# Third buffers, keys a head ahead, squares summed on TensorE, and a new woven order in a fused GDN, sparse-attention and MLP layer

## The chip, the cores and the metric

One core of a Trainium2 chip runs the whole layer in one launch. The metric is device time in microseconds (us) of an execution; lower is better. Five engines run side by side, each through its own instructions in order: PE (TensorE, matmuls), ACT (ScalarE), DVE (VectorE), POOL (GpSimd) and SP (SyncE, which issues most transfers).

## The reference, cut to what matters

One decoder block over 1024 positions of width 1024. The piece that the change touches is the gated DeltaNet branch (GDN): 8 heads of 128, chunks of tokens, a short causal convolution, l2-normalised q and k, a decay, and a triangular solve.

```python
h = rms_norm(x, norm_mix_g)
proj = h @ w_in
qkv = silu(causal_short_conv(g_qkv, conv_w))          # 4 taps
gq = l2_normalize(gq) * 128 ** -0.5                   # x * rsqrt(sum(x*x) + EPS)
gk = l2_normalize(gk)
beta = sigmoid(g_b); g = -exp(a_log) * softplus(g_a + dt_bias)
decay = exp(g_cum[i] - g_cum[j])                      # i >= j
a_mat = (k_beta @ k.T) * decay                        # i > j
sol = triangular_solve(I + a_mat, [v * beta, k_beta * exp(g_cum)])
for each chunk n:                                     # the scan
    v_new = u_n - w_n @ state
    o_n = q_n @ state + qk_n @ v_new
    state = state * exp(g_last) + k_n.T @ v_new
o_gdn = rms_norm(o_gdn) * silu(z)
o_att = sparse attention over the 256 best keys of an indexer
x = x + (sigmoid(gate_a) * o_gdn + sigmoid(gate_b) * o_att) @ w_out
x = x + relu(rms_norm(x) @ w_mlp_up) ** 2 @ w_mlp_down
```

## The kernel before, in words

**Tiling and stages.** Tokens are cut into 8 blocks of 128 (`NB`, `P`). The core first normalises x, then projects the indexer, the attention operands and the decay scalars (the start, about the first 270 us), then runs the GDN heads with the indexer's top-k search beside them (to about 1000 us), the attention, the output projection, and from about 1258 us the MLP.

**The dense stream.** The GDN weights are cut into 48 units (`gunits`, L659): for each head k, q, v (convolved), z and gate a, and for all heads gate b. `gload` (L668) fetches a unit's raw weights, `gweights` (L674) splits them on ACT and DVE into a high and a low part (tiles `w`), and `gdense` (L696) runs 2 halves of 24 matmuls each of 128x512 into PSUM tiles `dd`. A half may begin only when the same half of the unit before has been drained, by `conv` or `gate`, on ACT (`cu<-dd`, `th<-dd`). These matmuls are the filler of the order: anything else that PE has to do is put between them.

**A head's chain.** `conv` (L745) copies the two halves into `cu` (2 buffers), scales and adds the four taps (`kt`, `qt` or `t`), takes tanh into `cu` on ACT and finishes silu on DVE. From k, `keys` (L786) fetches the cumulated decay into `es` by a broadcast DMA (`es<-GC`), transposes the eight blocks of k on PE (`tt<-kt`, `tt<-ident,kt`), takes the sum of squares of each with an ACT Square that accumulates (`gj,kss<-tt`) and the decayed keys `kd` with a second ACT instruction, turns `es` into the decay with ACT's Abs and Exp (`es<-es,ngc`), and makes the matrix `am`. POOL then inverts the 32x32 diagonal blocks in 31 steps (`stmp`, `sx`), with two round trips through DRAM (`ZA`, `ZU`) into `um`. `join` (L887) puts the blocks together with small matmuls (`jj`). From q, `queries` (L941) transposes 8 blocks only to sum squares in the same way (`qss`), then multiplies k and q into `es`. `values` (L975) transposes v (`vv`), `scan` (L997) runs 8 dependent steps (`cc`, `oo`, `sr`, `svn`, `sst`) and `output` (L1050) norms and gates the result. `es`, `kd` and `um` have two buffers each, so `keys` of head h waits for the scan of head h-2 before it does anything.

**What sets the order.** Nothing is ordered by hand. Every piece is a generator chain with a priority (`wv.add`), and `Weave` (L1608) plays the chains against a model of durations (`__getattr__`, L1694) and issues whichever may run. `issue` (L1622) ties each instruction to the one before it on its engine, so that the order planned at build time is the order on the chip: an instruction whose data come later than planned holds up everything behind it on its engine. All instructions carry the line of that wrapper, L1699, so that a reader goes by tile names.

Of the kernel before, what the change touches and what calls it, by code (L numbers as in the profile page):

```python
# [20 lines left out]
P = 128  # L21
# [8 lines left out]
TOPK = 256  # L30
NEG = -1.0e30
# [18 lines left out]
def body(tc, a, out, dbg=None):  # L50
# [67 lines left out]
    cmask = cst.tile([P, P], F32, name="cmask")  # L118
    vecs = cst.tile([P, NV], F32, name="vecs")
    g025 = cst.tile([P, 1], F32, name="g025")  # L120
    dtb = cst.tile([P, H], F32, name="dtb")
# [25 lines left out]
    def loads():  # L147
        SY_.dma_start(ident, a["c_ident"])
        after(("ident",))
        for half in range(2):  # L150
            if half == 0:
                ts = [ix.tile([P, NB, 256], F32, name="pj", bufs=2).rearrange("p a b -> p (a b)") for _ in range(2)]
                xs.extend(t[:, o:o + D] for t in ts for o in (0, D))
            else:
                xs.extend([slot(1, [P, D], F32), slot(5, [P, D], F32)]
                          + [ix.tile([P, D], F32, name="irl", bufs=2) for _ in range(2)])
            for tb in range(4 * half, 4 * half + 4):
                SY_.dma_start(xs[tb], x[tb * P:(tb + 1) * P, :])
# [15 lines left out]
        G_.memset(ones, 1.0)  # L174
        SY_.dma_start(ropeA, a["c_ropea"])
        SY_.dma_start(qng, a["q_norm_g"].to_broadcast([P, P]))
        SY_.dma_start(kng, a["k_norm_g"].to_broadcast([P, P]))
        SY_.dma_start(cmask, a["c_mask"])
        yield
# [418 lines left out]
    def select():  # L598
# [29 lines left out]
        for qb in range(2):  # L628
            m = scp.tile([P, 2, P], BF16, name="tkcm")
            G_.memset(m[:, 0, :], 0.0)  # L630
            G_.tensor_copy(m[:, 1, :], cmask)
            yield
            SY_.dma_start(MK[qb, :, :(qb + 1) * P], m[:, 1 - qb:, :])
# [21 lines left out]
    gunits = []  # L655
# [6 lines left out]
    graws = [None, None]  # L662

    def wtile(kind, u):
        i = {"r": (2, 3), "h": (6, 0), "l": (7, 4)}[kind][u % 2]
        return slot(i, [P, KT, P], F32 if kind == "r" else F32R)

    def gload(u):  # L668
        h, c = gunits[u]
        c0 = cstart[c] + h * P  # L670
        graws[u % 2] = wtile("r", u)
        SY_.dma_start(graws[u % 2], w_in[:, c0:c0 + P].rearrange("(k p) c -> p k c", p=P))

    def gweights():  # L674
        yield ("pdense", len(units) - 2)
        gload(0)
        gload(1)
        for u in range(len(gunits)):
            yield
            if u == 1:  # L680
                yield ("pdense", len(units) - 1)
            if u > 1:
                yield ("dense", u - 2)
            yield "A"
            hi, lo = wtile("h", u), wtile("l", u)
            A_.activation(hi, graws[u % 2], AF.Copy)
            yield
            yield "V"
            V_.tensor_tensor(lo, graws[u % 2], hi.bitcast(F32), op=OP.subtract)
# [55 lines left out]
    def conv(u):  # L745
# [14 lines left out]
        if c == "k" and h > 2:  # L760
            yield ("out", h - 3)
        if c == "q" and h > 1:
            yield ("scan", h - 2)
        if c == "v" and h:
            yield ("values", h - 1)
# [14 lines left out]
        yield  # L780
        wv.done("conv", u)
        st[h][c + "t"] = o
# [3 lines left out]
    def keys(h):  # L786
        kt = st[h]["kt"]
        if h > 1:
            yield ("scan", h - 2)
        kd = gp.tile([P, NB, P], F32, name="kd", bufs=2)  # L790
        es = gp.tile([P, NB, P], F32, name="es", bufs=2)
        am = gq.tile([P, NB, P], F32, name="am", bufs=2)
        um = gp.tile([P, NB, P], F32, name="um", bufs=2)
        kss = gp.tile([P, NB], F32, name="kss", bufs=2)
# [3 lines left out]
        for half in range(2):  # L798
            yield tt.ready
            ps, slot_ = tt.get()  # L800
            for i in range(4):
                PE_.transpose(ps[:, i, :], blk(kt, half * 4 + i), ident)
            yield
            for i in range(4):
# [4 lines left out]
                if i % 2:  # L809
                    yield  # L810
            tt.free(slot_)
# [8 lines left out]
        ke = gp.tile([P, NB], F32, name="ke", bufs=2)  # L820
        V_.tensor_scalar(ke, kss, 4 * EPS, None, op0=OP.add)
        yield
        yield from rsq_w(gp, rk, ke, NB, "rk")
# [29 lines left out]
        st[h].update(kd=kd, aq=es, am=am, av=av, nb=nb_, um=um)  # L853
# [32 lines left out]

    def join(h):  # L887
# [8 lines left out]
        ys = gq.tile([P, NB, 32], F32, name="ys", bufs=1)  # L896
# [26 lines left out]
        y6 = gq.tile([64, NB, 64], F32, name="y6", bufs=1)  # L923
# [17 lines left out]
    def queries(h):  # L941
        qt = st[h]["qt"]
        yield ("keys", h)
        if h > 1:
            yield ("out", h - 2)
        kt, aq = st[h]["kt"], st[h]["aq"]
        qss = gp.tile([P, NB], F32, name="qss", bufs=2)
        for half in range(2):
            hs = slice(half * 4, half * 4 + 4)
            yield tt.ready  # L950
            ps, slot_ = tt.get()
            for i in range(4):
                PE_.transpose(ps[:, i, :], blk(qt, half * 4 + i), ident)
            yield
            for i in range(4):
                b = half * 4 + i
                junk = gp.tile([P, P], BF16, name="gj")
                A_.activation(junk, ps[:, i, :], AF.Square, accum_out=qss[:, b:b + 1])
                if i % 2:
                    yield  # L960
            tt.free(slot_)
# [9 lines left out]
        st[h]["qss"] = qss  # L971
        wv.done("queries", h)
# [24 lines left out]
    def scan(h):  # L997
        yield ("queries", h)
        yield ("values", h)
        if h:  # L1000
# [49 lines left out]
    def output(h):  # L1050
# [4 lines left out]
        V_.tensor_scalar(fe, qss, 4 * EPS, 128 * EPS, op0=OP.add, op1=OP.mult)  # L1055
# [52 lines left out]
    xslot = (1, 5, 2, 3, 6, 7, 0, 4)  # L1108
# [72 lines left out]
    def wout_weights():  # L1181
        free = [("V", 1), ("out", H - 1), ("w", last), ("w", last), ("dense", last - 1), ("dense", last - 1)]
# [425 lines left out]
class Weave:  # L1608
    def __init__(self, tc):
        self.tc, self.now, self.idle, self.t = tc, 0.0, 0.0, 0.0  # L1610
        self.busy, self.last, self.ev, self.chains = {}, {}, {}, []
# [10 lines left out]
    def issue(self, name, ins, dur, lat):  # L1622
# [5 lines left out]
        end = max(self.busy.get(name, 0.0), self.now) + dur  # L1628
# [61 lines left out]
class _Ordered:  # L1690
    def __init__(self, wv, eng, name):
        self.wv, self.eng, self.name = wv, eng, name

    def __getattr__(self, op):  # L1694
# [3 lines left out]
        def call(*args, **kw):  # L1698
# [5 lines left out]
            if name == "PE":  # L1704
# [3 lines left out]
                if op == "matmul" and "tile_position" in kw:  # L1708
                    return wv.issue(name, ins, 0.03, 0.25)
                return wv.issue(name, ins, (n * (0.417 if fast else 0.835) + 2.5) / 1e3, 0.25)  # L1710
            if name == "SY":
                return wv.issue(name, ins, max(0.5, n * o.shape[0] / 9e4), SY_LATENCY)
            if name == "A":
                return wv.issue(name, ins, 0.13 + n / 1200 + (0.1 if "accum_out" in kw else 0), 0.15)
            if name == "V":
                return wv.issue(name, ins, 0.07 + n / 960, 0.12)
            if op == "tensor_tensor":
                return wv.issue(name, ins, 0.33 + n / 476, 0.2)
            return wv.issue(name, ins, 0.15 + n / 1000, 0.2)
# [3 lines left out]
def constants():  # L1723
# [4 lines left out]
    c["c_mask"] = np.where(i[None, :] <= i[:, None], 0.0, NEG).astype(np.float32)  # L1728
# [42 lines left out]
```

## Time and profile before

| what | before |
|---|---|
| median of 3 runs | 1967.49 us (1966.48 to 1968.16) |
| the profiled execution, its own time | 1966.45 us |
| its span | 1964.7 us |
| mean granted clock of TensorE | 0.987 of full speed |
| PE, DVE, ACT, POOL busy | 1917.2, 1045.0, 890.6, 374.3 us |
| instructions | 27845, of them 10526 on PE |

PE's rows are records of matmuls: a float32 product of two 128x128 tiles leaves two records, a transpose one. Their ends are modelled and overlap, so that the distance from one start to the next tells more than a mean duration. A stretch in which PE's clock falls from 1.00 to 0.50 runs its matmuls at half speed. The time between span and execution, 1.75 us, lies around the span.

### The profile page before, as it was taken

To read this page: it belongs to the slowest core of one execution; us is meant where nothing else is said; L and a number is where in the kernel's file an instruction comes from. 1 tells how busy PE (TensorE), PEld (TensorE's weight loads), DVE (VectorE), ACT (ScalarE), POOL (GpSimd) and SP (SyncE) were. 2 spreads that over 40 slices of the span, in tenths; PEclk is the share of its full clock that TensorE was granted. 3 is DMA by queue.
4 is the path that set the end of the run, shared out by engine and by line. 5 is a ranking of instruction groups with operands and counts; after the bars stand their busy time and mean duration, and the time that the engine had idled before them with its cause. 6 is when DMAs were issued, how large, how long until landed. Compare 5 with 4: busy or idle time off the path is not lost.

```text
span 1964.7 us, 27845 instructions
## 1 busy us (share of the span) xinstructions
PE 1917.2 (98%) x10526; PEld 1613.2 (82%) x10526; DVE 1045.0 (53%) x2371; ACT 890.6 (45%) x2022; POOL 374.3 (19%) x661
## 2 busy tenths in 40 slices
PE   8899999999999799999999999999999999999999
PEld 7899988887887688888877888788888888888887
DVE  4547767767868786543377766623223232223222
ACT  6556657657655535543365655532221314132220
POOL 0214721540650533531021221000000000000000
PEclk9999999998999899999999999999999999999999
DMA  4111243212322222223362211212020211112012
GB/s 152 45 43 44 83 122 60 65 47 62 64 58 46 60 71 78 56 69 92 97 221 92 71 61 49 76 38 59 32 81 17 70 43 43 48 38 60 32 33 91
DMA packets 181689, 131.17 MB, mean 67 GB/s; under 512 B 34306, under 2 KB 161715, under 8 KB 181555
## 3 DMA queue, kind: packets, MB, share of 16 engines
q1 hardware_dynamic: 181554, 129.40, 23.1%
q8 instruction: 82, 1.34, 0.3%
q14 instruction: 53, 0.43, 0.1%
HBM read 107.18 MB, written 22.18 MB: 66 GB/s over the span
## 4 chain that ended last, share of the span: by engine, by line
PE 93%; DVE 3%; ACT 3%; DMA 1%; issue 1%; SPq 0%; ACTq 0%; DVEq 0%
PE dd L1699 58%; PE o L1699 11%; PE pt L1699 11%; PE s L1699 3%; PE tt L1699 3%; PE cc L1699 2%; PE jj L1699 2%; PE sq L1699 2%; PE oo L1699 1%; DVE rqs L1699 1%; ACT pr L1699 1%; DVE sc L1699 0%; PE tp L1699 0%; DMA es<-GC 0%; DMA pj<-in_x_dram 0%
## 5 line engine op out<-in xcount | busy, mean ns | idle before, releaser
L1699 PE MATMUL dd<-hh,w 128*128 128x512 f32 x1568 | 526.6, 407 | 2.6 <-ACT cu L1699 1.6
L1699 PEld LDWEIGHTS dd<-hh,w 128*128 128x128 f32 x1568 | 292.5, 190 | 59.6 <-ACT cu L1699 2.8
L1699 PE MATMUL dd<-hl,w 128*128 128x512 f32 x784 | 319.1, 407 | 0.9 <-DVE hl L1699 0.9
L1699 PE MATMUL dd<-w,hh 128*128 128x256 f32 x960 | 181.6, 286 | 0.0
L1699 PEld LDWEIGHTS dd<-hl,w 128*128 128x128 f32 x784 | 149.2, 190 | 28.1 <-DVE hl L1699 1.2
L1699 ACT ACTIVATE dh<-dr 128x512 fp32r<-128x512 f32 x64 | 40.2, 628 | 280.3 <-PE o L1699 230.4
L1699 PEld LDWEIGHTS dd<-w,hh 128*128 128x128 f32 x960 | 153.0, 192 | 1.5
L1699 ACT ACTIVATE rl<-dd 128x512 f32<-128x512 f32 x64 | 38.3, 598 | 218.6 <-PE dd L1699 218.6
L1699 PE MATMUL dd<-w,hl 128*128 128x256 f32 x480 | 137.0, 285 | 0.0
L1699 POOL TENSOR_TENSOR stmp<-sx,um 128x60 f32<-128x60 f32 (+24 forms) x248 | 109.9, 443 | 99.0 <-DMA sx<-in_c_xinit_dram 80.8
L1699 DVE TENSOR_TENSOR w<-w,o 128x512 f32<-128x512 f32 x64 | 44.0, 688 | 126.4 <-PE o L1699 126.4
L1699 DVE TENSOR_SCALAR_CACHE_REDUCE tkeq<-sc,cand 128x384 f16<-128x384 f32 (+3 forms) x128 | 103.5, 808 | 1.5
L1699 PE MATMUL dd<-h2h,uh 128*128 128x512 f32 x256 | 100.7, 393 | 1.3 <-DVE w L1699 1.3
L1699 POOL TENSOR_TENSOR sx<-sx,stmp 128x60 f32<-128x60 f32 (+24 forms) x248 | 98.2, 396 | 19.4
L1699 PE MATMUL dd<-hh,ul 128*128 128x512 f32 x256 | 100.4, 392 | 0.0
L1699 PE MATMUL dd<-h2l,uh 128*128 128x512 f32 x256 | 100.4, 392 | 0.0
L1699 PE MATMUL dd<-hh,uh 128*128 128x512 f32 x256 | 100.3, 392 | 0.0
L1699 PE MATMUL dd<-h2h,ul 128*128 128x512 f32 x256 | 100.3, 392 | 0.0
L1699 PE MATMUL dd<-hl,uh 128*128 128x512 f32 x256 | 100.3, 392 | 0.0
L1699 DVE TENSOR_TENSOR w<-w,pt 128x512 f32<-128x512 f32 x64 | 44.0, 688 | 102.1 <-PE pt L1699 101.0
L1699 PEld LDWEIGHTS dd<-w,hl 128*128 128x128 f32 x480 | 91.9, 191 | 0.1
L1699 DVE TENSOR_TENSOR dl<-dr,dh 128x512 fp32r<-128x512 f32 x64 | 44.0, 688 | 84.3 <-ACT dh L1699 84.3
(366 smaller groups left out, 4384.4 us busy)
## 6 DMA issues: line engine op xcount, KB each, us to landing
w<-in_w_in_dram SPq DMA_DIRECT2D x48, 512.0 KB, 3.9
ur<-in_w_mlp_up_dram SPq DMA_DIRECT2D x32, 512.0 KB, 4.3
dr<-in_w_mlp_down_dram SPq DMA_DIRECT2D x64, 256.0 KB, 2.8
wraw<-in_w_in_dram SPq DMA_DIRECT2D x8, 1024.0 KB, 5.3
w<-in_x_dram SPq DMA_DIRECT2D x10, 512.0 KB, 5.1
es<-GC SPq DMA_DIRECT2D x8, 512.0 KB, 9.1
um<-ZA SPq DMA_DIRECT2D x32, 128.0 KB, 3.9
M<-kt SPq DMA_DIRECT2D x8, 512.0 KB, 2.8
```

What stands on the lines that cost most here:

```text
L1699: ins = f(*args, **kw)
```

## The change

- **Buffers.** `es` gets a third buffer; the third `um`, for every third head, takes the large slot 3. For that the raw GDN weights get one slot (2) instead of two (2, 3): a unit's weights are now fetched when the unit before it has been split. The decayed keys with their k transposes become a chain of their own, `decayed`. `keys` now waits for the scan of head h-3 and the join of head h-2.
- **Units.** The k unit of each head goes a head ahead in `gunits`, and two gate b units (`EARLY`) go behind head 0's.
- **Squares.** The accumulating ACT Squares of k (64) and q (64) and the 64 transposes of q go. In their place `conv` of k and of q squares the whole tile in one ACT instruction into `cu`, and PE multiplies each of its 8 blocks, as the stationary operand, by a 128x1 column of ones; a DVE addition of EPS takes the sums out of PSUM.
- **The planner.** Its price of a matmul column goes from 0.417 to 0.441 ns, the fixed part from 2.5 to 5 ns, wide small matmuls cost 0.06 us, two POOL prices fall slightly, and DVE and POOL instructions with two operands in SBUF are planned one after another (`port`).
- **Smaller ones.** The causal mask is made on POOL rather than loaded, `ys` and `y6` of `join` live in free blocks of `am`, and the slots in which the attention and the output weights wait are renumbered.

```diff
...
-    for h in range(H + 1):
-        gunits += [(h, c) for c in "kqv" if h < H] + [(h - 1, c) for c in "za" if h]
-    gunits += [(h, "b") for h in range(H)]
+    gunits = [(0, "k"), (0, "q"), (0, "v"), (1, "k")]
+    for h in range(H):
+        gunits += [(g, c) for g, c in ((h + 1, "q"), (h + 1, "v"), (h + 2, "k")) if g < H] + [(h, "z"), (h, "a")]
+        if h == 0:
+            gunits += [(g, "b") for g in range(EARLY)]
+    gunits += [(h, "b") for h in range(EARLY, H)]
...
-        i = {"r": (2, 3), "h": (6, 0), "l": (7, 4)}[kind][u % 2]
+        i = {"r": (2, 2), "h": (6, 0), "l": (7, 4)}[kind][u % 2]
...
-            if u + 2 < len(gunits):
-                gload(u + 2)
+            if u + 1 < len(gunits):
+                gload(u + 1)
...
+        st[h][c + "t"] = o
+        if c != "v":
+            yield "A"
+            A_.activation(cu[:, 0:S], o, AF.Square)
+            yield
+            yield tt.ready
+            ps, slot_ = tt.get()
+            for b in range(NB):
+                PE_.matmul(ps[:, 0, b:b + 1], blk(cu, b), one, start=True, stop=True)
+            yield
+            st[h][c + "ss"] = gp.tile([P, NB], F32, name=c + "ss", bufs=3)
+            V_.tensor_scalar(st[h][c + "ss"], ps[:, 0, 0:NB], 4 * EPS, None, op0=OP.add)
+            tt.free(slot_)
+            yield
         wv.done("conv", u)
...
     def keys(h):
         kt = st[h]["kt"]
+        if h > 2:
+            yield ("scan", h - 3)
         if h > 1:
-            yield ("scan", h - 2)
-        kd = gp.tile([P, NB, P], F32, name="kd", bufs=2)
-        es = gp.tile([P, NB, P], F32, name="es", bufs=2)
+            yield ("join", h - 2)
+        es = gp.tile([P, NB, P], F32, name="es", bufs=3)
-        um = gp.tile([P, NB, P], F32, name="um", bufs=2)
-        kss = gp.tile([P, NB], F32, name="kss", bufs=2)
+        um = slot(3, [P, NB, P], F32) if h % 3 == 2 else gp.tile([P, NB, P], F32, name="um", bufs=2)
+        wv.add(3, decayed(h))
...
-                A_.activation(junk, ps[:, i, :], AF.Square, accum_out=kss[:, b:b + 1])
-                A_.activation(kd[:, b, :], ps[:, i, :], AF.Copy, scale=egd[:, b, h:h + 1])
...
+    def decayed(h):
+        if h > 1:
+            yield ("scan", h - 2)
+        kd = gp.tile([P, NB, P], F32, name="kd", bufs=2)
+        for half in range(2):
+            yield tt.ready
+            ps, slot_ = tt.get()
+            for i in range(4):
+                PE_.transpose(ps[:, i, :], blk(st[h]["kt"], half * 4 + i), ident)
+            yield
+            for i in range(4):
+                b = half * 4 + i
+                A_.activation(kd[:, b, :], ps[:, i, :], AF.Copy, scale=egd[:, b, h:h + 1])
...
     def queries(h):
...
-                PE_.transpose(ps[:, i, :], blk(qt, half * 4 + i), ident)
-            yield
-            for i in range(4):
-                b = half * 4 + i
-                junk = gp.tile([P, P], BF16, name="gj")
-                A_.activation(junk, ps[:, i, :], AF.Square, accum_out=qss[:, b:b + 1])
...
-                    return wv.issue(name, ins, 0.03, 0.25)
-                return wv.issue(name, ins, (n * (0.417 if fast else 0.835) + 2.5) / 1e3, 0.25)
+                    return wv.issue(name, ins, 0.03 if n <= 32 * NB else 0.06, 0.25)
+                return wv.issue(name, ins, (n * (0.441 if fast else 0.835) + 5) / 1e3, 0.25)
...
```

**The order on PE, where head 1 is joined.** Before (`dd` are the dense matmuls, `jj` those of the join, `tt<-ident,vv` the transposes of v, `cc<-vv,um` the first step of head 1's scan, x4 stands for four alike):

```order
L1699 MATMUL jj<-ys,t_4976 32x32 x16
L1699 MATMUL jj<-t_4976,ys 32x32 x8
L1699 MATMUL dd<-hl_1_124,w_4701 128x512
L1699 MATMUL dd<-hh_1_108,w_4702 128x512
L1699 MATMUL jj<-um,am 64x64 x8
L1699 MATMUL jj<-y_5092,t_4976 64x64 x8
L1699 MATMUL tt<-ident,vv 128x128 x4
L1699 MATMUL cc<-vv,um 128x128
L1699 MATMUL tt<-ident,vv 128x128 x4
L1699 MATMUL cc<-svn,kd 128x128
L1699 MATMUL oo<-svn,es 128x128
L1699 MATMUL dd<-hh_0_93,w_4876 128x512
```

With the change, where the scan of head 0 ends and head 1 is joined (`tt<-one,cu` are the new sums of squares):

```order
L1727 MATMUL cc<-sr,um 128x128
L1727 MATMUL oo<-svn,es 128x128
L1727 MATMUL tt<-ident,kt 128x128 x8
L1727 MATMUL jj<-um,am 32x32 x16
L1727 MATMUL jj<-am,t_4978 32x32 x16
L1727 MATMUL jj<-t_4978,am 32x32 x8
L1727 MATMUL jj<-um,am 64x64 x8
L1727 MATMUL jj<-am,t_4978 64x64 x8
L1727 MATMUL tt<-one,cu 128x1 x8
L1727 MATMUL tt<-ident,vv 128x128 x4
L1727 MATMUL cc<-vv,um 128x128
L1727 MATMUL dd<-hh_0_93,w_4706 128x512
```

The last dense matmul ahead of this piece stands six rows earlier; the piece begins with the last step of head 0's scan, then come the output's transposes, the whole join, a burst of ones and the first step of head 1. Before, dense matmuls of one unit lay between the join's steps; now there is none up to the last row.

**The order on PE, where head 3's v is transposed.** Before (`tt<-ident,kt` is the output of the head before, `cc` and `oo` are steps of the scan):

```order
L1699 MATMUL dd<-hh_1_108,w_6937 128x512
L1699 MATMUL cc<-sst,kt 128x128
L1699 MATMUL oo<-sst,qt 128x128
L1699 MATMUL cc<-sr,um 128x128
L1699 MATMUL oo<-svn,es 128x128
L1699 MATMUL tt<-ident,kt 128x128 x8
L1699 MATMUL tt<-ident,vv 128x128 x4
L1699 MATMUL dd<-hh_0_93,w_7184 128x512
```

With the change:

```order
L1727 MATMUL tt<-ident,vv 128x128 x4
L1727 MATMUL dd<-hh_1_108,w_7278 128x512
L1727 MATMUL jj<-am,t_7528 32x32 x16
L1727 MATMUL jj<-t_7528,am 32x32 x8
L1727 MATMUL dd<-hl_1_124,w_7278 128x512
L1727 MATMUL dd<-hh_1_108,w_7279 128x512
L1727 MATMUL dd<-hh_0_93,w_7450 128x512
L1727 MATMUL dd<-hl_0_109,w_7450 128x512
```

Before, six rows stand between two dense matmuls; now the transposes of v and two steps of a join stand between dense matmuls.

**The order on ACT, ahead of head 4's decay** (`es<-es,ngc` is its Abs, `kd<-tt,egd` the decayed keys, `gj,kss<-tt` the squares of k, `cu<-qt` and `cu<-kt` the tanh of a convolution or the new square, `svn<-cc` and `gj,oss<-vv` steps of a scan). Before:

```order
L1699 ACTIVATE gj,kss<-tt 128x128
L1699 ACTIVATE kd<-tt,egd 128x128
L1699 ACTIVATE um<-jj 64x8x64
L1699 ACTIVATE gj,kss<-tt 128x128
L1699 ACTIVATE kd<-tt,egd 128x128
L1699 ACTIVATE gj,kss<-tt 128x128
L1699 ACTIVATE kd<-tt,egd 128x128
L1699 ACTIVATE cu<-qt 128x1024
L1699 ACTIVATE svn<-cc 128x128
L1699 ACTIVATE es<-es,ngc 128x128 x4
L1699 ACTIVATE cu<-dd 128x512
L1699 ACTIVATE gj,oss<-vv 128x128
```

With the change:

```order
L1727 ACTIVATE cu<-kt 128x1024
L1727 ACTIVATE svn<-cc 128x128
L1727 ACTIVATE tkcm,cnt<-sc_154,cand 128x896
L1727 ACTIVATE tkcm,cnt<-sc_155,cand 128x1024
L1727 ACTIVATE gj,oss<-vv 128x128
L1727 ACTIVATE sqs<-oo,eg 128x128
L1727 ACTIVATE th<-dd 128x512
L1727 ACTIVATE svn<-cc 128x128
L1727 ACTIVATE es<-es,ngc 128x128 x2
L1727 ACTIVATE gj,oss<-vv 128x128
L1727 ACTIVATE es<-es,ngc 128x128 x2
```

The pairs of `gj,kss` and `kd` that stood between the transfer's issue and the Abs are gone; the scan, the search (`tkcm`) and the gates (`th<-dd`) stand there now, and the Abs comes in pairs between them.

## Rows read from the trace of the kernel before

**Rows 1.** The page: busy time by engine, and the chain that ended last by engine.

```profile
PE 1917.2 (98%) x10526; PEld 1613.2 (82%) x10526; DVE 1045.0 (53%) x2371; ACT 890.6 (45%) x2022; POOL 374.3 (19%) x661
...
PE 93%; DVE 3%; ACT 3%; DMA 1%; issue 1%; SPq 0%; ACTq 0%; DVEq 0%
```

**Rows 2.** Stretches: window, length, busy us (instructions) by engine, clock, DMA share, GB/s.

```profile
50.00:100.00 50.00, 42.20 (x317) 40.34 (x315) 29.18 (x66) 25.02 (x45) 10.22 (x5) 0.97 0.19 56
...
705.00:1000.00 295.00, 295.00 (x1885) 247.77 (x1885) 151.43 (x325) 131.90 (x373) 89.81 (x205) 1.00 0.29 81
1000.00:1050.00 50.00, 44.79 (x230) 34.41 (x228) 38.01 (x101) 36.28 (x77) 17.22 (x13) 0.97 0.64 217
1258.00:1961.00 703.00, 702.97 (x3040) 571.23 (x3040) 210.34 (x288) 181.07 (x284) 0.00 (x0) 1.00 0.16 50
```

**Rows 3.** The same view, three holes among the heads.

```profile
452.00:462.00 10.00, 6.95 (x48) 5.87 (x48) 7.48 (x19) 9.32 (x26) 0.10 (x1) 0.65 0.28 86
462.00:472.00 10.00, 10.00 (x45) 8.41 (x45) 8.34 (x34) 6.23 (x15) 0.00 (x0) 0.84 0.06 22
612.00:622.00 10.00, 6.90 (x53) 5.59 (x54) 7.94 (x16) 8.89 (x30) 0.10 (x1) 0.84 0.25 62
655.00:660.00 5.00, 2.33 (x14) 1.60 (x12) 4.33 (x12) 1.99 (x5) 4.22 (x11) 0.98 0.15 32
660.00:665.00 5.00, 2.38 (x10) 1.98 (x10) 4.69 (x14) 3.94 (x19) 4.41 (x10) 0.50 0.47 127
665.00:670.00 5.00, 1.06 (x4) 0.71 (x4) 4.86 (x9) 3.79 (x15) 4.61 (x6) 0.50 0.23 53
670.00:675.00 5.00, 4.34 (x13) 3.53 (x13) 3.53 (x8) 4.58 (x10) 4.06 (x13) 0.50 0.13 51
675.00:680.00 5.00, 5.00 (x19) 3.95 (x19) 3.64 (x8) 0.19 (x1) 4.29 (x11) 0.82 0.16 59
```

**Rows 4.** The chain of waits, 655 to 673: start, us, what.

```profile
660.70 8.15 DMA es<-GC
...
668.88 1.28 ACT es L1699 x4
670.15 0.49 ACT cu L1699
...
670.69 1.22 PE dd L1699 x2
```

**Rows 5.** PE's timeline near 86 us: start, us, instruction.

```profile
86.34 0.39 PE L1699 MATMUL sq<-ikl,iqt 128*128 128x512 f32 x1
86.57 0.22 PE L1699 MATMUL sq<-ikh,iqt 128*128 128x128 f32 x1
86.63 0.28 PE L1699 MATMUL sq<-ikl,iqt 128*128 128x128 f32 x1
86.75 0.34 PE L1699 MATMUL dd<-w,hh 128*128 128x256 f32 x1
```

**Rows 6.** The chain of waits, eight 128-column transposes and small matmuls of a join.

```profile
695.12 0.89 PE tt L1699 x8
...
605.50 1.02 PE jj L1699 x32
```

**Rows 7.** Groups by form, 280 to 1000 us: busy us, mean ns, idle before and releaser.

```profile
L1699 PE MATMUL tt<-ident,qt 128*128 128x128 f32 x64 | 9.6, 273 | 0.0
...
L1699 ACT ACTIVATE gj<-tt 128x128 bf16<-128x128 f32 x128 | 36.3, 284 | 13.3 <-PE tt L1699 11.7
...
L1699 ACT ACTIVATE cu<-qt 128x1024 f32<-128x1024 f32 x8 | 8.6, 1069 | 1.5 <-DVE qt L1699 1.5
...
L1699 DVE SCALAR_TENSOR_TENSOR qt<-cu,vecs,qt 128x1024 f32<-128x1024 f32 x24 | 30.8, 1282 | 4.1 <-ACT qt L1699 4.0
```

**Rows 8.** The page's transfers: issues, KB each, us to landing.

```profile
w<-in_w_in_dram SPq DMA_DIRECT2D x48, 512.0 KB, 3.9
```

**Rows 9.** PE's waits: engine line waited for, us in total, times, longest.

```profile
PE tp L1699 <- DVE iqs L1699: 5.2, 2, 3.5
```

More of the change, by code (lines that the diff above doesn't have):

```diff
@@ L30 @@
 TOPK = 256
+EARLY = 2
 NEG = -1.0e30
@@ L117, in body @@
     ident = cst.tile([P, P], F32, name="ident")
-    cmask = cst.tile([P, P], F32, name="cmask")
     vecs = cst.tile([P, NV], F32, name="vecs")
     g025 = cst.tile([P, 1], F32, name="g025")
+    one = cst.tile([P, 1], F32, name="one")
     dtb = cst.tile([P, H], F32, name="dtb")
@@ L174, in loads @@
         G_.memset(ones, 1.0)
+        G_.memset(one, 1.0)
         SY_.dma_start(ropeA, a["c_ropea"])
@@ L761, in conv @@
             yield ("out", h - 3)
+        if c == "k" and h > 1:
+            yield ("keys", h - 2)
         if c == "q" and h > 1:
             yield ("scan", h - 2)
+        if c == "q" and h > 2:
+            yield ("out", h - 3)
         if c == "v" and h:
@@ L819, in keys @@
         rk = gp.tile([P, NB], F32, name="rk", bufs=2)
[L820 to L823, printed above, removed]
+        yield from rsq_w(gp, rk, st[h]["kss"], NB, "rk")
         ck = gp.tile([P, NB], F32, name="ck", bufs=2)
@@ L884, in keys @@
         wv.add(1, join(h))
+    def decayed(h):
[11 more added lines that the diff above has]
+                A_.activation(kd[:, b, :], ps[:, i, :], AF.Copy, scale=egd[:, b, h:h + 1])
+                if i % 2:
+                    yield
+            tt.free(slot_)
+        st[h]["kd"] = kd
+        wv.done("decayed", h)
     def join(h):
@@ L999, in scan @@
         yield ("values", h)
+        yield ("decayed", h)
         if h:
@@ L1181, in wout_weights @@
     def wout_weights():
-        free = [("V", 1), ("out", H - 1), ("w", last), ("w", last), ("dense", last - 1), ("dense", last - 1)]
+        free = [("scan", 5), ("V", 1), ("w", last), ("out", H - 1), ("dense", last - 1), ("dense", last - 1)]
         stage = []
@@ L1610, in __init__ @@
         self.tc, self.now, self.idle, self.t = tc, 0.0, 0.0, 0.0
-        self.busy, self.last, self.ev, self.chains = {}, {}, {}, []
+        self.busy, self.last, self.ev, self.chains, self.port = {}, {}, {}, [], []
     def engine(self, eng, name):
@@ L1620, in done, with issue @@
         self.ev[key] = self.now
-    def issue(self, name, ins, dur, lat):
+    def issue(self, name, ins, dur, lat, port=False):
         prev = self.last.get(name)
@@ L1627, in issue @@
         self.last[name] = ins.ins.name
-        end = max(self.busy.get(name, 0.0), self.now) + dur
+        start = max(self.busy.get(name, 0.0), self.now)
+        if port:
+            self.port = [i for i in self.port if i[1] > self.now]
+            for a, b in self.port:
+                if start + dur <= a:
+                    break
+                start = max(start, b)
+            self.port = sorted(self.port + [(start, start + dur)])
+        end = start + dur
         self.busy[name] = end
@@ L1692, in __init__, with port @@
         self.wv, self.eng, self.name = wv, eng, name
+    def port(self, op, args, kw):
+        if self.name == "G":
+            return op != "memset"
+        ins = [t for t in args[1:] if hasattr(t, "shape")] + [kw[k] for k in ("in0", "in1") if k in kw]
+        if op in ("tensor_tensor", "scalar_tensor_tensor", "tensor_tensor_reduce"):
+            return sum(t.space != PSUM for t in ins if t.shape[1:] != (1,)) > 1
+        return op in ("tensor_scalar", "tensor_copy") and ins[0].space != PSUM and "accum_out" not in kw
     def __getattr__(self, op):
@@ L1714, in call @@
                 return wv.issue(name, ins, 0.13 + n / 1200 + (0.1 if "accum_out" in kw else 0), 0.15)
+            port = self.port(op, args, kw)
             if name == "V":
-                return wv.issue(name, ins, 0.07 + n / 960, 0.12)
+                return wv.issue(name, ins, 0.07 + n / 960, 0.12, port)
             if op == "tensor_tensor":
-                return wv.issue(name, ins, 0.33 + n / 476, 0.2)
-            return wv.issue(name, ins, 0.15 + n / 1000, 0.2)
+                return wv.issue(name, ins, 0.3 + n / 476, 0.15, port)
+            return wv.issue(name, ins, 0.15 + n / 1000, 0.2, port)
         return call
```

48 lines of the change are left out of this document (12 added, 36 removed).

## The prediction

> **What bounds the kernel now.** I read the page first, then the clock and busy time by stretch, then the chain of waits inside the few stretches that are not full, and last PE's own rows. The page says that PE is busy for 1917.2 us and that 93% of the chain that ended last is PE [rows 1]. By stretch that is plainer: in the MLP PE is busy for 702.97 of 703 us at full clock, and from 705 to 1000 us for all of 295 [rows 2]. There a microsecond of work taken off PE is a microsecond gained, one added is lost, and what any other engine saves is worth nothing. Only holes can be gained otherwise. A hole costs its idle time and the busy time that ran below full clock, so I count idle + busy x (1 - clock). Three lie among the GDN heads [rows 3]: 452 to 472 us, 3.05 + 6.95 x 0.35 + 10 x 0.16 = 7.1 us; 612 to 622, 3.1 + 6.9 x 0.16 = 4.2 us; 655 to 680, 9.9 idle + 4.8 of slow clock = 14.7 us; together 26.0. Two lie elsewhere: 50 to 100 us in the start, 7.8 + 1.3 = 9.1, and 1000 to 1050 us where the attention begins, 5.2 + 1.3 = 6.5 [rows 2]. The longest hole has its cause in its chain: the transfer of the decay, `es`, takes 8.15 us, ACT's Abs stands behind it in ACT's order, the copy `cu` that drains the dense half stands behind the Abs, and the next dense matmul behind the copy [rows 4].
>
> **The squares: dearer on PE.** 16 convolutions (q and k of 8 heads) now make 8 matmuls each with 128x128 stationary blocks and one moving column. A float32 product of this kind leaves two records, so 16 x 8 x 2 = 256 records. Before has no one-column matmul, so I bound it. From above: a 128-column pass behind another 128-column pass starts the next after 0.12 us, 86.63 to 86.75 [rows 5], or 0.89 / 8 = 0.111 in a run of transposes [rows 6]. From below: products of 32x32 tiles pass in 1.02 / 32 = 0.032 us [rows 6], so 256 x 0.032 = 8.2. The rows between tell which is nearer: the same 128-column pass took 0.06 us where its stationary block could be loaded under a 512-column one, and 0.12 where only a short pass lay ahead [rows 5]. So half of 0.12 is no streaming of columns; it is the change of the 128x128 block, and each ones matmul brings a new block with nothing long beside it. I take 0.111: 256 x 0.111 = **+28.4 us**, at most 256 x 0.12 = 30.7. Out go 64 transposes of q, one record each [rows 7], 64 x 0.111 = **-7.1 us**. Those of k stay, for `kd`. Net **+21.3** (from +1.1 to +23.6).
>
> The Trainium skill, "TensorE: Matmul & The Clock Gate", has two rules for this that no run here has yet decided between. Its section "LDWEIGHTS (loading the stationary operand)" gives a load of P columns as P/1.2 ns whatever the rows and the moving columns, 107 ns for 128; an estimate by it is 256 x 0.107 = 27.3 us, which speaks against the change. Its table under "Back-to-back issue gap" gives a floor of about 25 ns for 1 to 64 columns, an estimate of 6.4 us. The 0.12 behind a short pass [rows 5] agrees with the first.
>
> What this frees is ACT: 36.3 us of Squares over 128x128 go, and 16 of 128x1024 come, about 1.07 each by the tanh of the same size, 17.1 [rows 7]. ACT is busy for 45% of the span [rows 1], covered by PE; so nothing, other than in the holes.
>
> **The old holes.** With three `es` buffers the transfer no longer waits for a scan's last step, and the k of a head is there a head earlier. In the order at head 3's transposes of v there were six rows without a dense matmul, and now there is dense work between; the other heads after the first are woven in the same way. I take all three holes as gone: **-26.0** (bounds -11.3, if the longest stays, and -26.0).
>
> **A new hole.** At the end of head 0's scan and the join of head 1 the order now puts 16 rows on PE without a dense matmul, the last eleven of which are shown with the change. PE's own work there is short: 7 scan products x 2 x 0.111 = 1.6, 8 transposes 0.9, 40 products of 32x32 x 2 x 0.032 = 2.6, 16 of 64x64 at 1 to 2, the ones 16 x 0.111 = 1.8, and 0.7 for v and the first scan step: about 9 us. What the last of these rows wait for is longer. The ones need the whole convolution of a q whose last dense half ended just ahead: copy 0.49 [rows 4], scale, tanh and Square 3 x 1.07 on ACT, three taps and silu 4 x 1.28 on DVE [rows 7], the ones 1.8, then v and the scan step 0.7: 11.3 us if nothing else stood on ACT and DVE. But the scan's steps, the join's copies and a weight split stand there too, and in the longest old hole DVE was busy for 13.9 of 15 us from 655 to 670 [rows 3]. So I expect about 20 us for 9 of work, and the clock falls in it as it did to 0.50 there. The nearest row is that old hole: 14.7. I take **+15** (bounds 4.2, the shortest old hole, and 20: 11 idle and 9 of work at half clock).
>
> **Smaller terms.** In the start PE waited 5.2 us for `iqs`, the scaled index queries [rows 9]; the new order puts some 2.7 us more dense work ahead of that wait and the clock may stay up: **-4** (0 to -9.1, the whole loss of that stretch). Late in the heads ACT's Abs of `es` now follows without the `gj`, `kd` pairs that covered the 8.15 us transfer [rows 4]; scan and search stand there instead. If the transfer is late, what is behind it on ACT is the drain of the dense half, and PE waits: **+3** (0 to 8.15 for a whole uncovered transfer). The raw weights have one slot: they are fetched when the unit before is split, land after 3.9 us [rows 8], and a unit's dense work lasts 48 x 0.23 = 11 us [rows 5]; hidden, unless SP or the split is late, then up to 3.9 a unit. `decayed`, the mask, `ys` and `y6` move without adding to PE: nothing. The attention's hole and the MLP keep their order: 0.
>
> **Sum**, against the profiled execution of 1966.45 us: +21.3 - 26.0 + 15 - 4 + 3 = +9.3, so 1975.8. The median of the runs is 1.04 above that execution: **1977 us**, some 0.5% slower.
>
> **Rivals.**
> 1. *Ones matmuls are cheap*: what counts is the moving column, 0.032 a record [rows 6]. Then +1.1 in place of +21.3: about 1957. For it: small products do pass so fast. Against: those have small stationary blocks too, and rows 5. This is the side of the floor in the skill's "Back-to-back issue gap" ("TensorE: Matmul & The Clock Gate"). Chance 0.18.
> 2. *The new hole is short*: ACT and DVE run the q convolution ahead of the rest and PE waits only as in the shortest old hole, 4.2 in place of 15 [rows 3]: 1966, no change. For it: 9 us of PE work do lie in it. Against: that the shortest had dense work beside its join. Chance 0.18.
> 3. *ACT is held at every later head* by a transfer that nothing covers, or single raw weights come late: 4 us at five heads in place of 3 in all: 1977 + 17 = 1994. For it: ACT works in order, and rows 4 show the whole mechanism. Against: with a third buffer the transfer is issued early. Chance 0.11.
> 4. *The third buffer does nothing for the longest hole*, since the scan of a head still follows the join of the next: 14.7 stay: 1992. Against: the order there. Chance 0.05.
>
> **How the numbers follow.** The forecast case has 0.48, with a range of its own from 1972 to 1984 (the hole from 10 to 20, the ones up to 0.12). A measurement of this kernel tells about 0.2%, 3.9 us, from no change. Faster takes nearly all of rival 1 (0.16), a third of rival 2 (0.06) and little of the forecast case: 0.24. Same takes half of rival 2 and a part of the forecast case: 0.22. Slower has the rest, 0.54. The range reaches down to rival 1 and up to rivals 3 and 4, and leaves out their far halves: 1955 to 1992.
>
> **What would show it.** Right: `tt<-one,cu` starts 0.11 apart in bursts of 1.7 to 1.9 us; 655 to 680 has no twin; one hole of 8 to 12 idle us, with a clock of 0.50, between the last dense matmul of a q unit and the next, ended by the ones; PE's busy time up by about 20 where it is full. Wrong: ones 0.06 apart or less; a PE that runs full past head 1's join; dense matmuls late in the heads that wait for `cu` or `w`.

## The result, and the profile after

| what | before | after |
|---|---|---|
| median | 1967.26 us (1966.48 to 1968.16, 4 runs) | 1984.14 us (1981.39 to 1986.61, 4 runs) |
| the profiled execution | 1966.45 us | 1981.92 us |
| its span | 1964.7 us | 1980.2 us |

The ratio is 1.0085, with an interval of 1.0067 to 1.0103: the kernel is slower by 0.7 to 1.0%. The forecast was 1977 in a range of 1955 to 1992, and slower.

The page of the kernel after, beside [rows 1]: PE still is 98% of the span and 93% of the chain, with 24 us more of it.

```profile
PE 1941.2 (98%) x10718; PEld 1630.9 (82%) x10718; DVE 1031.0 (52%) x2379; ACT 870.6 (44%) x1782; POOL 383.3 (19%) x662
...
PE 93%; DMA 2%; ACT 2%; DVE 1%; issue 1%; POOL 1%; SPq 0%; POOLq 0%; ACTq 0%; DVEq 0%
```

**The ones.** PE's timeline of the kernel after, from the start of a burst of ones to the dense pass behind it:

```profile
279.65 1.84 PE L1727 MATMUL tt<-one,cu 128*128 128x1 f32 x16
281.35 0.71 PE L1727 MATMUL dd<-hh,w 128*128 128x512 f32 x2
```

16 records in 281.35 - 279.65 = 1.70 us, 0.106 each; 16 bursts are 27.2 us at full clock. The forecast had 28.4.

**The new hole.** Busy time by stretch around the join of head 1, in the columns of [rows 2], kernel after:

```profile
440.00:450.00 10.00, 6.82 (x33) 5.04 (x31) 8.60 (x28) 5.30 (x13) 0.64 (x1) 0.85 0.28 50
450.00:455.00 5.00, 4.18 (x43) 3.69 (x42) 3.15 (x11) 3.73 (x12) 0.29 (x2) 0.50 0.79 192
455.00:460.00 5.00, 1.94 (x43) 1.94 (x44) 4.94 (x17) 2.99 (x6) 4.29 (x10) 0.50 0.00 0
460.00:465.00 5.00, 2.98 (x30) 2.65 (x28) 4.72 (x10) 3.46 (x7) 4.41 (x10) 0.50 0.00 2
465.00:470.00 5.00, 5.00 (x31) 4.88 (x30) 0.06 (x1) 0.93 (x2) 4.04 (x13) 0.50 0.01 3
470.00:475.00 5.00, 4.15 (x17) 3.66 (x17) 1.97 (x8) 1.66 (x5) 4.00 (x13) 0.50 0.00 0
475.00:480.00 5.00, 5.00 (x22) 4.22 (x21) 1.16 (x5) 1.77 (x4) 3.97 (x15) 0.73 0.27 107
```

Idle plus busy x (1 - clock) gives 4.2, 2.9, 4.0, 3.5, 2.5, 2.9 and 1.4: 21.4 us, 9.9 of them idle. PE's timeline in it:

```profile
458.06 1.57 PE L1727 MATMUL jj<-am,t 32*32 32x32 f32 x29 [3.51 <-ACT am L1727]
...
466.34 3.57 PE L1727 MATMUL tt<-one,cu 128*128 128x1 f32 x16
```

The idle time lies ahead of the scan's last steps and of the join's, the longest of it 3.51 us for the join's copy `am` on ACT, and 0.85 ahead of the dense half at the end. The ones waited for nothing: PE went straight on to them from the join. From 465 to 470 PE is busy for all of 5 us and loses half of them all the same, since the burst runs there at half clock: 3.43 us to the next start at 469.77, 0.214 a record. The chain of waits at the hole's end, and ACT's timeline:

```profile
466.41 4.46 PE tt L1727 x20
...
471.61 0.49 ACT cu L1727
...
472.14 0.79 PE dd L1727
```

```profile
451.86 1.13 ACT L1727 ACTIVATE qt<-cu,vecs 128x1024 f32<-128x1024 f32 x1
...
471.33 0.28 ACT L1727 ACTIVATE svn<-cc 128x128 f32<-128x128 f32 x1 [4.29 <-PE cc L1727]
471.50 1.08 ACT L1727 ACTIVATE cu<-dd 128x512 f32<-128x512 f32 x2
```

The dense half waits to be drained by `cu<-dd`. ACT is idle for 4.29 us ahead of it, because in its order the copy stands behind `svn`, which waits for the first step of head 1's scan, and that stands behind the ones on PE. `conv` lets a convolution begin when the one two before it is done, and with the change it is done only after its ones; so the planner puts the copy there. The convolution is q's of head 2. By the order of the units its halves were copied by 415 us, but its first step (`qt<-cu,vecs`) runs only at 451.86, since in the code it waits for the scan of head 0 while it holds a buffer of `cu`. Both rules are read from the code and the order; no run changed either.

**The old holes and the start.** The same view, kernel after; the stretches of [rows 3] and the attention's of [rows 2]:

```profile
612.00:622.00 10.00, 10.00 (x136) 8.20 (x136) 8.31 (x19) 4.14 (x9) 1.76 (x1) 1.00 0.47 132
650.00:700.00 50.00, 49.50 (x312) 41.03 (x312) 36.95 (x114) 20.80 (x51) 11.80 (x26) 1.00 0.26 54
...
1000.00:1050.00 50.00, 44.58 (x218) 33.80 (x217) 40.86 (x94) 35.51 (x65) 16.34 (x11) 1.00 0.73 239
```

The start, kernel before (beside the row of 50 to 100 us in [rows 2]) and kernel after:

```profile
0.00:50.00 50.00, 41.32 (x249) 36.68 (x250) 23.79 (x52) 31.09 (x45) 4.69 (x8) 0.93 0.46 150
...
100.00:150.00 50.00, 49.36 (x349) 47.50 (x350) 23.65 (x35) 30.91 (x69) 5.76 (x4) 0.93 0.10 30
150.00:200.00 50.00, 48.33 (x372) 46.56 (x371) 41.41 (x59) 29.60 (x66) 23.83 (x17) 1.00 0.13 43
```

```profile
0.00:50.00 50.00, 41.04 (x247) 36.03 (x248) 23.69 (x52) 30.99 (x45) 4.56 (x9) 0.90 0.46 148
50.00:100.00 50.00, 49.16 (x387) 47.77 (x387) 30.77 (x69) 28.77 (x50) 10.71 (x5) 1.00 0.21 65
100.00:150.00 50.00, 50.00 (x378) 48.23 (x377) 31.31 (x36) 30.66 (x71) 17.66 (x14) 1.00 0.07 22
150.00:200.00 50.00, 50.00 (x388) 48.60 (x387) 28.97 (x51) 33.38 (x92) 24.55 (x17) 1.00 0.27 85
```

The old holes at 612 and 655 us are gone but for half a microsecond; the one at 452 lay where the new one is, and what is lost there now is counted in the new one. The start loses 13.1 + 0.8 = 13.9 us, where it lost 11.6 + 9.1 + 4.1 + 1.7 = 26.5: a gain of 12.6. The attention's stretch loses 5.4 after 6.5.

Ones +27.2, transposes -7.1, old holes -26.0, new hole +21.4, start -12.6, attention -1.1: together +1.8, and the profiled executions differ by 15.5. Idle time in the heads adds 4.9 (540 to 860 us, rows with the first run), and 2.0 more is idle behind the attention: +8.7. The 6.8 us that are left are in no row of the change, and the fifth and sixth runs below are for them.

### The profile page after: what moved, and what is told of

The parts are those of the page before. It is cut to its first block, busy times and chain, and to the rows that moved or that the text cites. A ratio compares the mean times of both kernels' runs of the same rounds, so it can differ in the third digit from the quotient of the medians.

```text
span 1980.2 us, 27946 instructions
## 1 busy us (share of the span) xinstructions
PE 1941.2 (98%) x10718; PEld 1630.9 (82%) x10718; DVE 1031.0 (52%) x2379; ACT 870.6 (44%) x1782; POOL 383.3 (19%) x662
## 4 chain that ended last, share of the span: by engine, by line
PE 93%; DMA 2%; ACT 2%; DVE 1%; issue 1%; POOL 1%; SPq 0%; POOLq 0%; ACTq 0%; DVEq 0%
PE dd L1727 57%; PE o L1727 11%; PE pt L1727 11%; PE tt L1727 4%; PE s L1727 3%; PE sq L1727 2%; PE jj L1727 2%; PE cc L1727 2%; DMA es<-GC 2%; PE oo L1727 1%; ACT es L1727 1%; PE tp L1727 0%; DMA pj<-in_x_dram 0%; POOL hl L1727 0%; DVE w L1727 0%
## 5 line engine op out<-in xcount | busy, mean ns | idle before, releaser
L1727 POOL TENSOR_TENSOR stmp<-sx,um 128x60 f32<-128x60 f32 (+24 forms) x186 | 76.3, 410 | 77.3 <-DMA sx<-in_c_xinit_dram 63.9
```

The lines of the kernel that those rows point to most:

```text
L1727: ins = f(*args, **kw)
```

## The experiments

The theory: the ones are paid in full for the change of a 128x128 block, the new hole is made by the planned order, and the third buffers took the old holes away. The rivals: the ones lie beside other work; the hole lies in the data; the buffers do nothing.

**1. Squares in bf16.**

```diff
-    one = cst.tile([P, 1], F32, name="one")
+    one = cst.tile([P, 1], BF16, name="one")
-            A_.activation(cu[:, 0:S], o, AF.Square)
+            sb = cu.bitcast(BF16)[:, 0:S]
+            A_.activation(sb, o, AF.Square)
-                PE_.matmul(ps[:, 0, b:b + 1], blk(cu, b), one, start=True, stop=True)
+                PE_.matmul(ps[:, 0, b:b + 1], blk(sb, b), one, start=True, stop=True)
```

> The change, with the squares written as bf16 and multiplied by a bf16 column of ones; the order on every engine stays that of the change. The 256 records of 0.112 us (28.7 us) become 128, since a bf16 product leaves one. Theory, the price is the change of a 128x128 block for each record: at 0.11 a record 14.1 us, so 14.6 less, and the burst in the hole is shorter by some 2 us at half clock: about 1967. Rival, the price goes with the bytes of the block or with passes of the float32 product: 0.055 or less a record, 7 us, so 22 or more less: about 1960. A second rival, the ones cost nothing where they stand, because PE waits anyway: 1981 to 1986, as the change.

Measured: 1966.85 us (10 runs), 1.0006 of before [0.9997, 1.0015]. The time is the theory's, the reason the rival's. A burst and what follows on PE:

```profile
291.04 0.34 PE L1728 MATMUL tt<-one,cu 128*128 128x1 bf16 x8 [1.00 <-ACT cu L1728]
291.24 0.47 PE L1728 MATMUL dd<-hl,w 128*128 128x512 f32 x1
```

0.20 / 8 = 0.025 us a record, not 0.11: a bf16 block is far cheaper than a float32 one of the same shape. The bursts fell from 27.2 to 16 x 0.20 = 3.2, by 24 us, and the kernel gained 17. Some came back as waits. The heads by stretch, the change and then this run:

```profile
540.00:700.00 160.00, 156.99 (x988) 132.11 (x987) 113.45 (x324) 86.23 (x196) 62.74 (x134) 1.00 0.23 57
700.00:860.00 160.00, 158.15 (x1064) 132.95 (x1061) 112.99 (x263) 75.19 (x179) 64.38 (x136) 1.00 0.23 61
```

```profile
540.00:700.00 160.00, 155.01 (x1003) 128.61 (x1002) 114.07 (x318) 87.57 (x198) 60.68 (x135) 1.00 0.25 61
700.00:860.00 160.00, 155.37 (x1007) 129.31 (x1006) 117.61 (x268) 74.23 (x181) 61.80 (x130) 0.99 0.24 62
```

Idle time there grew from 4.9 to 9.6 us: a PE with less to do waits for ACT and DVE a little more. The hole at head 1's join stays, though the burst in it is now short:

```profile
440.00:480.00 40.00, 31.08 (x233) 27.25 (x234) 25.92 (x79) 23.40 (x60) 24.03 (x65) 0.66 0.19 48
```

8.9 us idle and 31.1 x 0.34 of slow clock are 19.5, beside 21.4 with float32 ones: the time of the ones does not make the hole.

**2. Ones twice.** The loop of eight matmuls is issued a second time.

> The change, with each burst of ones matmuls issued a second time into the same column. Theory, they are paid in full: 256 more records of 0.112 are 28.7 us, and up to 3.6 more in the hole at half clock: 2013 to 2017. Rival, most of the price is hidden in waits of PE: under 2000.

Measured: 2026.51 us, 1.0317 [1.0284, 1.0349], 42 more than the change. The rival falls. The theory was short by about 10, and the granted clock says where. A burst, the dense pass behind it, and a stretch at the end of the next burst but one, which lasts from 327.2 to 330.8 us:

```profile
281.10 3.63 PE L1729 MATMUL tt<-one,cu 128*128 128x1 f32 x32
...
284.58 0.71 PE L1729 MATMUL dd<-hh,w 128*128 128x512 f32 x2
```

```profile
330.00:335.00 5.00, 5.00 (x24) 4.32 (x24) 1.42 (x3) 0.00 (x0) 0.10 (x1) 0.66 0.41 109
```

32 records take 3.48 us, 0.109 each. In the stretch the clock falls to its lower level (0.66 in the mean) with PE busy for all of it. Such a fall comes in the burst or within 2 us of its end at 12 of the 16 doubled bursts; behind the 15 single bursts that the change ran at full clock there is none.

**3. Without the price of the shared port.** The three prices of DVE and POOL are those of before.

> The change without the planner's model of the port that DVE and POOL share (the two POOL prices as before, too); buffers, units, ones and matmul prices stay. In the order on PE no stretch without a dense matmul holds more than 2.6 us of PE work after the start, where the change has one of 9.3. Theory, the hole of 22.5 us at head 1's join is made by the order: about 1962, the ones still at 28.7. Rival, the hole lies in the data (the q convolution of head 2 waits for head 0's scan while it holds a buffer of cu), and no order helps: 1980 or more.

Measured: 1984.92 us, 1.0102 [1.0087, 1.0117], the time of the change. By stretch:

```profile
50.00:150.00 100.00, 89.45 (x647) 85.48 (x647) 56.25 (x99) 57.41 (x115) 15.48 (x9) 0.95 0.14 43
440.00:480.00 40.00, 40.00 (x312) 33.86 (x311) 32.65 (x82) 26.69 (x60) 22.09 (x54) 1.00 0.15 45
...
745.00:755.00 10.00, 4.89 (x24) 3.63 (x22) 1.73 (x3) 0.47 (x2) 0.56 (x2) 0.87 0.46 115
```

Half of the theory holds: the hole at the join is gone, 40 of 40 us at full clock, so it was not in the data. But the gain was given back: 15.0 us are lost from 50 to 150 us, where the change loses 0.8, and a new hole opens at 745 us, 5.7 us in its first ten, where PE's waits name the transfer behind the inverse (`jj` waits for `ZU`, 5.7 us). So the start's gain of the change hangs on the order that these prices bring.

**4. Old squares in the new order.** The transposes of q and the accumulating Squares come back, no ones.

> The change with the squares as before: transposes of q and accumulating Squares on ACT, no ones matmuls, the sum of k's squares taken beside the decayed keys; buffers, units and planner as in the change. In the order on PE a stretch of 9.1 us of work without a dense matmul stays at the same place. Theory, the squares are worth -28.7 + 7.1 = -21.6 and the hole stays: about 1962. Rival, the ones also make the hole, since they hold a buffer of cu: the hole falls below 10 us too and the time to about 1950. Second rival, the old squares cost as much on the path of ACT: 1975 or more.

Measured: 1993.87 us, 1.0141 [1.0124, 1.0158]: far from the theory and the first rival; the second rival's bound holds, though not by ACT's squares alone. There is less work on PE, and there are more holes; two of them by stretch:

```profile
600.00:660.00 60.00, 51.30 (x345) 42.91 (x343) 47.77 (x145) 30.31 (x91) 1.37 (x3) 0.86 0.18 38
750.00:800.00 50.00, 39.17 (x275) 33.45 (x274) 38.06 (x95) 23.73 (x72) 5.46 (x16) 0.83 0.16 40
```

They lose 15.9 and 17.5 us. Here the keys' sums also wait for the decayed keys, the column's tile goes and addresses with it (runs 5 and 6), and the whole order is planned anew, so the run tells no price of the squares; it tells that an order for one set of work is no order for another.

**5 and 6. Four bytes.** The change with the column taken from a wider tile, and the kernel before with one unused tile.

```diff
-    one = cst.tile([P, 1], F32, name="one")
+    one = cst.tile([P, 16], F32, name="one")[:, 0:1]
```

> The change with the column of ones taken from a tile of 64 bytes a partition rather than 4. The order on every engine stays; every tile that is placed behind it, the moving operands of the dense matmuls among them, moves by 32 bytes to an address of 32 modulo 64, as in the kernel before. In the trace of the change a 512-column dense pass takes 0.235 us from one to the next in the heads, before 0.232, and over all dense passes that is some 7 to 10 us of PE which no instruction explains. Theory, the address does it: 0.232 again, and 1984 - 8 = 1976. Rival, the passes are slower for another reason (what lies between them, the run): no change, 1982 to 1986.

```diff
     g025 = cst.tile([P, 1], F32, name="g025")
+    one = cst.tile([P, 1], F32, name="one")
...
         G_.memset(ones, 1.0)
+        G_.memset(one, 1.0)
```

> The kernel before with one unused tile of 4 bytes a partition ahead of the same operands, filled once on POOL; nothing else differs, and the order stays. The operands then stand at 0 modulo 64, as in the change. Theory of the address: dense passes of 0.235 us in the heads and 1966 + 8 = 1974. Rival: 1966.

Measured: the padded change 1973.36 us, 1.0037 [1.0024, 1.0050], 10.8 less than the change (9.4 by the two ratios to before); the shifted kernel before 1971.51 us, 1.0030 [1.0019, 1.0041], 4.9 more than before. The same passes in the chain of waits, one row each of before, of before shifted, of the change and of the change padded:

```profile
342.02 18.59 PE dd L1699 x80
```

```profile
343.77 18.74 PE dd L1701 x80
```

```profile
376.52 21.31 PE dd L1727 x91
```

```profile
373.61 21.23 PE dd L1727 x91
```

0.2324 to 0.2342 us a pass, and 0.2342 to 0.2333: 1 to 2 ns where the theory had 3. The pages of the shifted and of the padded kernel have the rest:

```profile
PE 1923.9 (98%) x10526; PEld 1614.0 (82%) x10526; DVE 1043.2 (53%) x2371; ACT 892.6 (45%) x2022; POOL 373.8 (19%) x662
```

```profile
PE 1932.4 (98%) x10718; PEld 1627.2 (83%) x10718; DVE 1030.4 (52%) x2379; ACT 872.7 (44%) x1782; POOL 381.8 (19%) x662
```

PE's busy time is 6.7 us more than before's 1917.2, and 8.8 less than the change's 1941.2, for the same PE instructions in the same order. So both runs went the theory's way, and the effect is in PE's work, in small steps all along the execution, the MLP too. In either pair nothing differs but addresses and, in the shifted kernel, one short fill on POOL. Which of the tiles that move matters was not tried.

**7. Both.** Run 1 with a padded column, `cst.tile([P, 32], BF16, name="one")[:, 0:1]`.

> The bf16 squares of the first run with the padded column. Theory, the two gains add: 1967 - 8 = 1959, clearly below the kernel before. Rival, the address does nothing: 1967.

Measured: 1957.9 us, 0.9961 [0.9946, 0.9976]. The gains add.

**8 and 11. More gate units early.** Run 7 with `EARLY = 4`, and with 3.

> As the run before this one, with four gate b units behind head 0's rather than two. In the order on PE the stretch of 9.3 us without a dense matmul at head 1's join becomes one of 2.9. Theory, the hole at head 1's join is for want of dense units that need no buffer of cu, and two more fill it: 1959 - 18 = 1941. Rival, the waits move to another head, as without the port's price, where 13.5 us went at 750 to 800 us: 1955 or more.

> The run with gate units early, with three of them. In the order the stretch at head 1's join holds 6.3 us of PE work, where two gates leave 9.3 and four 2.9. With four, 18 us went where the attention begins (950 to 1000 us), against about 9 with two, since the gates taken to the front are missing as filler there. Theory, each gate moved trades one hole for the other: between 1947.5 and 1958, about 1951. Rival, the hole at the join closes with three already and the attention's grows less: below 1945.

Measured: with four 1947.49 us, 0.9910 [0.9893, 0.9927]; with three 1954.54, 0.9941 [0.9924, 0.9957]. With four, by stretch:

```profile
440.00:480.00 40.00, 38.09 (x290) 31.20 (x289) 28.68 (x79) 24.44 (x56) 21.65 (x49) 1.00 0.18 45
...
950.00:1000.00 50.00, 38.84 (x174) 28.45 (x173) 30.13 (x82) 25.16 (x48) 6.96 (x5) 0.90 0.50 174
```

That is about midway between the theory and the rival. The hole at the join shrinks from 21.4 us in the change to 1.9, since gates are drained without a buffer of `cu`. But 15.0 are lost where the attention begins, for want of the same gates there. The trade is as the theory of the second run had it: three leave a hole at the join and open one at the attention.

**9. Old buffers.** Run 8 with two buffers for `es` and `um`, two raw weight slots, the old wait of `keys`, and the slots of the attention's and output's weights as before.

> The run with four gate units early (1947.5), with the buffers as before: two for the decay, two for um, two raw weight slots fetched two units ahead, and the keys of a head waiting for the scan two heads back. Theory, the third buffers are what took the 14.7 us hole away, whose chain was the transfer of the decay behind a scan's last step: it comes back, 1947 + 15 to 25, so 1962 to 1972. Rival, with the keys a head ahead and gates as filler two buffers do: 1944 to 1952.

Measured: 1997.51 us, 1.0162 [1.0146, 1.0177], 50 more than run 8. The direction is the theory's, the size is not. PE's waits (waited for, us in total, times, longest), two stretches, and ACT's Abs in the first of them:

```profile
PE tt L1727 <- ACT cu L1727: 24.5, 4, 12.9
```

```profile
600.00:640.00 40.00, 27.06 (x204) 22.77 (x202) 29.06 (x87) 23.09 (x49) 0.10 (x1) 0.74 0.23 60
...
1000.00:1050.00 50.00, 31.84 (x120) 22.03 (x118) 28.60 (x77) 23.44 (x44) 7.29 (x4) 0.73 0.46 158
```

```profile
616.87 0.69 ACT L1727 ACTIVATE es<-es,ngc 128x128 f32<-128x128 f32 x2 [2.15 <-DMA es<-GC]
```

In the first stretch 20.0 us go. PE stands at the ones from 614.30 to 627.24, 12.9 us, and waits for a Square. The transfer of the decay is part of the chain: ACT waited 2.15 us for it ahead of the Square, with the Abs and the Exp behind it. The second stretch loses 26.8 us where the attention begins; no ones stand there. The run changes the buffers, the slots and the wait of `keys` together, and the order is planned anew, so it doesn't tell which of them costs.

**10. New squares alone.** The kernel before with bf16 squares and the padded column.

> The kernel before with only the squares changed: a bf16 Square of the whole tile in the convolution, ones matmuls of bf16, the column padded so that addresses stay at 32 modulo 64. On PE -7.1 for the transposes of q and 128 x 0.025 = +3.2. Theory, the relief of ACT (128 Squares with their accumulators) is worth nothing beside a full PE: 1966.7 - 3.9 = 1963. Rival, ACT's squares lengthened every hole, as the run with the old squares in the new order suggests: 1955 or less. Second rival, the replanned order opens new holes (it has stretches of 5.2, 6.2 and 9.4 us of PE work without a dense matmul): 1967 or more.

Measured: 1968.42 us (10 runs), 1.0016 [1.0007, 1.0025]. The second rival: some 4 us less on PE, and more than that in holes of the new order, 14.1 us of them from 750 to 800 us, where the kernel before has none. No gain from the relief of ACT shows.

**12. The matmul prices alone.** The kernel before with

```diff
-                    return wv.issue(name, ins, 0.03, 0.25)
-                return wv.issue(name, ins, (n * (0.417 if fast else 0.835) + 2.5) / 1e3, 0.25)
+                    return wv.issue(name, ins, 0.03 if n <= 32 * NB else 0.06, 0.25)
+                return wv.issue(name, ins, (n * (0.441 if fast else 0.835) + 5) / 1e3, 0.25)
```

> The kernel before with the planner's matmul prices of the change alone (0.441 ns a column and 5 ns, 0.06 us for the wide small ones), so another order of the same instructions. After the start its order has no stretch without a dense matmul above 3.0 us of PE work. Theory, the holes at 452 and 612 us (7.1 and 4.2) were made by the order and go, the one at 655 (14.7) is made by the buffers and stays: 1966.7 - 11 = 1956. Rival, a stretch of the order says little, since waits move: within 5 us of 1967.

Measured: 1946.73 us, 0.9904 [0.9889, 0.9919]: some 9 us better than the theory. Its stretches where the old holes were:

```profile
450.00:472.00 22.00, 22.00 (x123) 18.64 (x122) 16.39 (x52) 16.39 (x43) 0.10 (x1) 1.00 0.24 73
600.00:650.00 50.00, 47.60 (x345) 40.62 (x344) 35.18 (x103) 27.13 (x87) 6.92 (x21) 0.93 0.24 62
650.00:700.00 50.00, 49.68 (x285) 40.98 (x284) 47.98 (x103) 26.07 (x73) 26.42 (x51) 1.00 0.35 89
```

The hole of 7.1 is gone, as the theory had it; that of 14.7 is gone too, with two buffers, which the theory had to stay; some 5.7 us are lost from 600 to 650. Nothing else of the change is in this kernel. It and run 8 beat both kernels and can't be told apart. What the two would give together was not tried.

## Why the prediction was right, and where its sizes were off

- **Ones, +28.4, and transposes, -7.1.** Right: 0.106 to 0.109 us a record, 27.2 us. The choice by the nearest row (a short float32 pass with a new 128x128 block) held, and rival 1 fell. By the Trainium skill, "TensorE: Matmul & The Clock Gate", "LDWEIGHTS (loading the stationary operand)", a block of 128 columns takes an estimated 107 ns (128/1.2); the float32 bursts at full clock agree with it, the one at half clock, 0.214, does not. The bf16 block does not either, at 0.025, and that is the floor for few columns in the Trainium skill's "TensorE: Matmul & The Clock Gate", "Back-to-back issue gap". The Trainium skill's section "Weight-path perf modes — Fast Weight Load (FWL) and DoubleRow" of the same title has a faster load for data other than float32, which fits; no run here parts the load from the passes.
- **Old holes, -26.0.** Right that they go. The reason was half wrong: the prediction gave the 14.7 us hole to the buffers, and run 12 closes it with two. In the new order of units run 9, with the buffers, slots and waits of before, is 50 us slower, and the transfer of the decay is in one of its holes; that the third buffers alone are needed there isn't shown.
- **New hole, +15.** Mis-sized: 21.4, above the upper bound of 20 that I set. Place and end were as forecast, a q convolution whose ones stand at the end, and it took about as long as forecast, 17.9 us from its first step to the last of the ones. Why it came so late was not: the forecast has its last dense half just ahead, and it had been held for the scan of head 0 since 415 us. The bound had 11 us idle and 9 of work at half clock; 9.9 were idle, but 11.5 went to the clock, which was low in the work ahead of the hole and behind it as well, from before 450 to after 475.
- **Start, -4.** Mis-sized: -12.6, beyond the -9.1 of the one stretch I looked at: 8.3 there and 4.1 and 1.7 in the two behind it, against 1.5 more lost in the first 50 us. By run 3 the gain hangs on the planner's prices of DVE and POOL, which the forecast did not look at.
- **ACT's late drains, +3.** Did not come: from 480 to 1000 us PE's waits name only `svn`, a step of the scan (4.8 us), never a copy to `cu`. The 4.9 us idle from 540 to 860 are that, so a number near +3 is luck.
- **Missing in the sum.** The addresses behind a tile of four bytes, 5 to 11 us. That column was in the diff, and the sum has no term for it. The 6.8 us that the rows leave open are of its size: PE's busy time moved by 6.7 and 8.8 in the two pairs.

The error of 7 us between 1977 and 1984 is thus the difference of larger ones: about +6 in the hole, +5 to 11 for the addresses, against -9 in the start. That they nearly cancel is luck; what was understood is the price of the ones, the place of the new hole, and that the old ones go.

## What to carry to other kernels

Where a planner fixes the order, its prices are part of the kernel: the matmul prices alone took the kernel before to 0.990, while the change, which has the same prices together with buffers, units and squares, came to 1.0085. Most gains elsewhere were partly taken back by a wait that the new order brought. Find what a new instruction costs before it is handed to a planner, above all one that changes a stationary block for a single column, and try it in bf16: the planner's formula has a ones matmul at 6.7 ns (1.67 a column and 5), and in float32 PE took 0.212 us for its two records. What a right price would give was not tried. After any change to the tiles ahead of a matmul's operands, compare the time of the same long run of passes; if it moved, pad.

## What the runs showed of the hardware that I had not expected

- A float32 product of a 128x128 block with one column took 0.106 to 0.109 us a record at full clock (0.214 in the one burst at half clock), two records each; in bf16 0.025 us and one record. For the same sums that is 27.2 against 3.2 us.
- A tile of 4 bytes a partition ahead of the operands made the kernel before 4.9 us slower, and 64 bytes in place of 4 made the change 9 to 11 us faster, with the same PE instructions in the same order.
- A busy PE lost its clock at 12 of 16 bursts of 3.48 us of one-column products (0.66 in the stretch from 330 to 335 us of run 2), and kept it behind the 15 bursts of 1.70 that the change ran at full clock.
